# Filler ahead of each recurrence, a norm in steps, and two projections on other PSUM banks

## The chip, the cores and the metric

The kernel runs on one core of a Trainium2 chip. The core has TensorE (PE, matrix products and transposes into PSUM), VectorE (DVE), ScalarE (ACT), GpSimd (POOL) and SyncE (SP), which issues the DMAs. Each engine runs its own instructions in order and waits for the others by semaphores. The metric is the time of one execution on the device in microseconds (us). PSUM, where TensorE writes, has eight banks; each holds a tile of 128 partitions x 512 float32.

## The reference

Two blocks run one after the other on a sequence of 1024 rows of 1024 columns. The change lies in the first part of the first block and at the beginning of its second part:

```python
def hybrid_mixer(h, w_in, ..., w_out):
    z = h @ w_in
    qkv, gate, a_logit, b_logit, cfm_in = jnp.split(z, [s1, s2, s3, s4], axis=-1)
    qkv = jax.nn.silu(causal_dwconv(qkv, gdn_conv_w))
    ...
    o = gated_delta_rule_chunked(q, k, v, g, beta)
    o = rmsnorm(o, gdn_norm_g) * jax.nn.silu(gate)
    c = jax.nn.glu(cfm_in, axis=-1)
    c = causal_dwconv(c, cfm_dw_w) + cfm_dw_b
    c = jax.nn.silu(layernorm(c, cfm_ln_g, cfm_ln_b))
    return jnp.concatenate([o_gdn, c], axis=-1) @ w_out

def memory_cross_attention(h, mem_n, w_q, w_kv, w_o):
    q = (h @ w_q).reshape(B, T, XATTN_HEADS, XATTN_HEAD_DIM)
    k, v = jnp.split(mem_n @ w_kv, 2, axis=-1)
    ...

y = hybrid_mixer(rmsnorm(h, g[0]), ...);  h = h + rmsnorm(y, g[1])
y = memory_cross_attention(rmsnorm(h, g[2]), rmsnorm(mem, mem_norm_g[l]), ...)
```

A gated linear unit with a short convolution and a second block of two more recurrences follow; they are the same in both kernels.

## The kernel before

**Products.** A float32 product is made of three matmuls on operands split into a high and a low part (`mm3`, L184 to L186): high by high, high by low, low by high, each 128 x 128 by 128 x 512. Activations are split as `x` (hi and lo), weights by `wunits`: a load of 512 KB on SP's queue brings `raw` (two buffers), ACT casts the high part `whi` (L149) and POOL, or VectorE in some places, subtracts to get `wlo` (L150), six buffers each. Each load gives two k-slices of a panel. At most LOOK = 3 loads are prepared ahead.

**PSUM.** The eight banks are four tagged `pa` (`A()`), two tagged `pm` (`M()`), and one each for `M(ns=0)` and `M(ns=1)`, which the trace shows as `pm` too. A projection panel takes four banks, one for each row tile (or column tile), and holds them over eight k-slices. Transposes of row norms go through the two banks of `M()`: `rows_to_T` transposes four 128x128 blocks into a bank (L229), ACT casts them to the high part and VectorE subtracts the low part. `banks()` returns the four of `A()` and the four others in turn.

**Stage 1.** The sequence is worked on in two halves of 512 rows (h = 0, 1), the four heads of the recurrence in two pairs (u = 0, 1). `weave(main, f, rate)` runs a recurrence `gdn_(h, u)` and takes `rate` filler steps of the generator `f` for each of its steps; what is left of the filler is then run to its end. A filler step of a projection is one `mm3`. A recurrence begins with squares of q and k (L551 on ACT), their sums by products with a column of ones (L553, 128x1), inverse roots in small steps on VectorE (L132 to L137), transposes (L571, L572) and decay products (L575); L459 gives the running sums of the log decay `glog` for both pairs of a half, in `s1_decay`. Its inputs come from `s1_qkv`: projections, a four-tap filter on VectorE (L385) and an activation (L386). The causal filter of 31 taps is L491 on VectorE. At the end of a recurrence L663 to L673 update the state and write the output.

**The order.** The program is written in one sequence, but a scheduler reorders it before it runs: it takes the written order as the priority, and for each engine puts next what it believes to be ready and to have a free buffer. The outcome is one fixed order for each engine.

**After the last recurrence** come the output projection of the first half (`out_`, two panels), its residual norm (`resid`: sums of squares L233, then L295 and L296), the row norm for the attention (`norm_T`: L308, then `rows_to_T`, 32 transposes), the output projection of the second half, whose two panels are copied out by L727, and `kv`, the projections of the memory to keys (two panels, 128x256 matmuls) and values (two panels, two row tiles each), which are split into `e` and `vl` by L149 and L150.

## Time and profile before

| | |
|---|---|
| median of 3 runs | 2958.16 us (2957.79 to 2959.43) |
| profiled execution | 2965.35 us, span 2963.5 us |
| mean granted clock of TensorE | 0.981 |
| busy: PE | 2806.0 us, 95% of the span |
| busy: DVE, POOL, ACT | 1778.4, 1241.0, 1125.8 us |
| DMA | 286.81 MB, mean 97 GB/s |

The profiled execution is one run; its trace gives the rows below. A row of the timeline has the start and the length of an instruction (or of a run of like ones, with its count), and in brackets how long the engine had been idle ahead of it and what ended that. A window's row has how long PE was busy in it and the granted clock as a share of full speed: 1.00 is the upper of two levels (2.4 GHz), 0.50 would be the lower one (1.2 GHz) throughout. Stage 1 lies between 0 and about 670 us: gdn(0,0) starts near 80 us, gdn(0,1) near 205, gdn(1,0) near 347, gdn(1,1) near 500; the output projection of the second half runs from 617 to 670, the keys and values from 675 to 731.

### The profile page before, as it was taken

Reading aid. Unit: us, or ns where it says so; the run is one execution under the profiler, and the core shown is the slowest. Engines: PE = TensorE matmul, PEld = TensorE weight load, DVE = VectorE, ACT = ScalarE, POOL = GpSimd, SP = SyncE. Lnnn points to the kernel's source line nnn. Section 1 sums busy time; section 2 is a strip of 40 time slices with the busy share of each in tenths; the row PEclk is TensorE's granted clock in tenths of the full one; section 3 lists DMA queues with packets and bytes.
Section 4 is the critical chain, followed back from the end, with each engine's and each line's share of the span. In section 5 each row is a group of like instructions: output and inputs, shape, how many; then the busy total and the mean of one; then the engine's idle time right before and its main releaser. Section 6 shows DMA issues by size and latency. Waiting matters only on the chain.

```text
span 2963.5 us, 40689 instructions
## 1 busy us (share of the span) xinstructions
PE 2806.0 (95%) x15268; PEld 2280.1 (77%) x15268; DVE 1778.4 (60%) x3525; ACT 1125.8 (38%) x2264; POOL 1241.0 (42%) x915
## 2 busy tenths in 40 slices
PE   7999998998999989999899998999999999999998
PEld 6787887877877778887688886777777777777776
DVE  6597789765345775546854547646546365464444
ACT  4443544555444443334333333323234322232333
POOL 3332333233342555554455543344443533434443
PEclk9999999999999999999899999999999999999999
DMA  4122111146242733334333234122223332222222
GB/s 152 43 65 72 50 44 58 36 136 199 70 136 83 244 113 94 99 93 160 129 98 100 91 94 160 61 86 65 86 79 99 93 123 70 79 61 90 79 78 100
DMA packets 136709, 286.81 MB, mean 97 GB/s; under 512 B 9793, under 2 KB 12865, under 8 KB 136513
## 3 DMA queue, kind: packets, MB, share of 16 engines
q1 hardware_dynamic: 136512, 284.22, 30.0%
q8 instruction: 120, 1.97, 0.3%
q14 instruction: 77, 0.62, 0.1%
HBM read 265.83 MB, written 18.35 MB: 96 GB/s over the span
## 4 chain that ended last, share of the span: by engine, by line
PE 52%; DVE 11%; DMA 3%; ACT 2%; issue 1%; POOL 1%; SPq 0%; ACTq 0%; DVEq 0%; POOLq 0%
PE pa L184 12%; PE pa L185 11%; PE pa L186 11%; PE pm L184 4%; PE pm L185 4%; PE pm L186 4%; PE pm L966 2%; DMA r<-h 1%; POOL wlo L150 1%; DMA wad<-in_w_ada 1%; DVE fo L833 1%; DVE mac L876 1%; DVE e L295 1%; PE pm L1023 0%; PE pm L1022 0%
## 5 line engine op out<-in xcount | busy, mean ns | idle before, releaser
L150 POOL TENSOR_TENSOR wlo<-raw,whi 128x512 fp32r<-128x512 f32 (+1 forms) x792 | 1145.8, 1453 | 1637.2 <-ACT whi L149 1614.0
L149 ACT CAST whi<-raw 128x512 fp32r<-128x512 f32 (+1 forms) x808 | 496.6, 620 | 1116.9 <-PE pa L186 515.8
L184 PE MATMUL pa<-whi,x 128*128 128x512 f32 (+2 forms) x1408 | 554.9, 395 | 12.8 <-DVE rt L1066 3.9
L186 PE MATMUL pa<-whi,x 128*128 128x512 f32 (+2 forms) x1408 | 546.2, 388 | 0.0
L185 PE MATMUL pa<-wlo,x 128*128 128x512 f32 (+2 forms) x1408 | 545.2, 387 | 0.0
L184 PE MATMUL pa<-x,whi 128*128 128x512 f32 x1024 | 428.5, 419 | 17.9 <-ACT x L1152 13.7
L185 PE MATMUL pa<-x,whi 128*128 128x512 f32 x1024 | 413.2, 403 | 0.0
L186 PE MATMUL pa<-x,wlo 128*128 128x512 f32 x1024 | 412.7, 403 | 0.0
L184 PEld LDWEIGHTS pa<-whi,x 128*128 128x128 f32 x1408 | 265.2, 188 | 75.2 <-issue 7.0
L186 PEld LDWEIGHTS pa<-whi,x 128*128 128x128 f32 x1408 | 265.1, 188 | 52.9 <-issue 0.9
L185 PEld LDWEIGHTS pa<-wlo,x 128*128 128x128 f32 x1408 | 265.4, 188 | 50.8 <-issue 1.4
L184 PEld LDWEIGHTS pa<-x,whi 128*128 128x128 f32 x1024 | 196.4, 192 | 58.3 <-ACT x L1152 14.5
L186 PEld LDWEIGHTS pa<-x,wlo 128*128 128x128 f32 x1024 | 195.9, 191 | 42.9
L185 PEld LDWEIGHTS pa<-x,whi 128*128 128x128 f32 x1024 | 196.6, 192 | 34.3 <-DVE x L150 0.4
L491 DVE SCALAR_TENSOR_TENSOR e<-padc,cw,e 128x512 f32<-128x512 f32 x240 | 202.4, 880 | 0.1
L828 DVE COPY fh<-pad 128x2 f32<-128x2 f32 x88 | 32.3, 367 | 227.3 <-ACT pad L826 227.3
L833 DVE SCALAR_TENSOR_TENSOR fo<-pad,cols,fo 128x512 f32<-128x512 f32 x176 | 159.8, 936 | 0.7
L184 PE MATMUL pm<-x,whi 128*128 128x512 f32 x384 | 154.5, 403 | 0.0
L185 PE MATMUL pm<-x,whi 128*128 128x512 f32 x384 | 152.9, 398 | 0.0
L186 PE MATMUL pm<-x,wlo 128*128 128x512 f32 x384 | 152.7, 398 | 0.0
L150 DVE TENSOR_TENSOR x<-pm,x 128x512 fp32r<-128x512 f32 x112 | 75.4, 687 | 66.4 <-ACT x L149 66.0
L149 ACT CAST x<-pm 128x512 fp32r<-128x512 f32 x112 | 64.6, 589 | 71.1 <-PE pm L229 42.6
(360 smaller groups left out, 4485.9 us busy)
## 6 DMA issues: line engine op xcount, KB each, us to landing
raw<-in_w_in SPq DMA_DIRECT2D x112, 512.0 KB, 3.9
raw<-in_ffn_w_up SPq DMA_DIRECT2D x88, 512.0 KB, 3.9
raw<-in_ffn_w_down SPq DMA_DIRECT2D x44, 512.0 KB, 3.9
raw<-in_w_out SPq DMA_DIRECT2D x32, 512.0 KB, 4.0
raw<-in_w_qf SPq DMA_DIRECT2D x32, 512.0 KB, 3.9
h<-e SPq DMA_DIRECT2D x48, 256.0 KB, 3.2
r<-h SPq DMA_DIRECT2D x24, 512.0 KB, 4.6
wad<-in_w_ada SPq DMA_DIRECT2D x24, 512.0 KB, 4.1
```

The lines of the kernel that those rows point to most:

```text
L149: self.nc.scalar.copy(hi, src)
L150: (lo_eng or self.nc.vector).tensor_tensor(lo, src, hi.bitcast(F32), ALU.subtract)
L184: mm(ps, lhsT=lh, rhs=rh, start=first, stop=False)
L185: mm(ps, lhsT=lh, rhs=rl, start=False, stop=False)
L186: mm(ps, lhsT=ll, rhs=rh, start=False, stop=last)
L295: nc.vector.scalar_tensor_tensor(yt, yt, r[:, t : t + 1], g[:, c], ALU.mult, ALU.mult)
L491: v.scalar_tensor_tensor(o, pad[:, k : k + HT], w(k), o, ALU.mult, ALU.add)
L828: v.tensor_copy(fh[:, i, :], pad[:, HT:])
L833: v.scalar_tensor_tensor(o, pad[:, k : k + HT], self.col(k0 + k), o, ALU.mult, ALU.add)
L876: v.scalar_tensor_tensor(ac, w, sc[:, k : k + 1], ac, ALU.mult, ALU.add)
L966: mm(pm[64 * e : 64 * e + 64, c, :], lhsT=kG[:, s], rhs=q[:, s], start=True, stop=True)
```

## The change

Four things are changed, all in the code that issues stage 1 and `kv`.

- `weave` gets a `lead`: so many steps of the filler are taken before the recurrence's first step. It is 8 for gdn(0,0) and 10 for gdn(0,1) and gdn(1,0); gdn(1,1) has none. With it, the decay (`s1_decay`) is no longer computed with the projection of its inputs but at the head of `gdn_(h, 0)`.
- The row norm of the second half of x, a call of `load_norm` ahead of gdn(0,1), becomes a generator `norm_steps`, of which one step is taken for every three steps of `conv_(0, 1)`.
- The first panel of the second half's output projection goes to the two banks of `M()` and those of `M(ns=0)` and `M(ns=1)` instead of `A()`.
- The four panels of `kv` take `banks()`, the two sets in turn, instead of `A()` each time.

```diff
+def beside(f, g, n):
+    for i, _ in enumerate(f):
+        yield
+        if i % n == n - 1:
+            next(g, None)
+    run(g)
...
-def weave(main, f, rate):
+def weave(main, f, rate, lead=0):
+    for _ in range(lead):
+        next(f, None)
     due = 0.0
...
-        return self.s1_decay(g) + (bt,)
+        return g, bt
...
-    def out_stream(self, y, xh, xl):
-        ps = [self.A() for _ in range(NTT)]
+    def out_stream(self, y, xh, xl, ps=None):
+        ps = ps or [self.A() for _ in range(NTT)]
...
-            ps = self.proj_T(units, xh, xl, nt=256)
+            ps = self.proj_T(units, xh, xl, nt=256, ps=self.banks())
...
-            ps = self.proj_R(units, xh, xl, ntt=2)
+            ps = self.proj_R(units, xh, xl, ntt=2, ps=self.banks())
...
             def gdn_(h, u):
+                if u == 0:
+                    dec[h] = self.s1_decay(dec[h][0]) + dec[h][1:]
                 yield from self.gdn(u, qkv[h, u], dec[h], gate[h])
 
             run(qkv_(0, 0, x))
-            weave(gdn_(0, 0), fill(conv_(0, 0, x), qkv_(0, 1, x)), RATE[0])
-            xn = self.load_norm(a["x"][HT:, :], gb(0))
-            weave(gdn_(0, 1), fill(conv_(0, 1, x), qkv_(1, 0, xn)), RATE[1])
-            weave(gdn_(1, 0), fill(conv_(1, 0, xn), norm_(0), conv_(1, 1, xn), qkv_(1, 1, xn)), RATE[2])
+            weave(gdn_(0, 0), fill(conv_(0, 0, x), qkv_(0, 1, x)), RATE[0], 8)
+            xn = self.X(), self.X()
+            norm = self.norm_steps(a["x"][HT:, :], gb(0), *xn)
+            weave(gdn_(0, 1), fill(beside(conv_(0, 1, x), norm, 3), qkv_(1, 0, xn)), RATE[1], 10)
+            weave(gdn_(1, 0), fill(conv_(1, 0, xn), norm_(0), conv_(1, 1, xn), qkv_(1, 1, xn)), RATE[2], 10)
             weave(gdn_(1, 1), fill(mix_(0), out_(0), norm_(1)), RATE[3])
             weave(mix_(1), out_(0), 4)
             self.resid(0, y[0], 0, 1)
             xa = self.norm_T(y[0], gb(2))
-            run(out_(1), out_(1))
+            run(out_(1, [self.M(), self.M(), self.M(ns=0), self.M(ns=1)]), out_(1))
...
+    def norm_steps(self, src, g, xh, xl):
+        hs = []
+        for t in range(NTT + 1):
+            if t < NTT:
+                hs.append(self.R())
+                self.nc.sync.dma_start(hs[t], src[t * P : (t + 1) * P, :])
+                self.prenorm([hs[t]], g, None, None)
+                yield
+            if t:
+                hr = hs[t - 1]
+                self.rows_to_T([hr[:, :HT], hr[:, HT:]], xh, xl, t - 1)
+                yield
```

The lines from L75 to L727 that are named here have numbers 11 higher in the changed kernel.

**PE at the start of gdn(0,1).** The long matmuls (`pa`, 128x512) are filler; L571 and L572 are the recurrence's first transposes (L582 and L583 in the changed kernel), L553 its sums of squares (now L564), L229 the norm's transposes (now L240). Before:

```order
L185 MATMUL pa<-x_131,whi 128x512
L186 MATMUL pa<-x_130,wlo 128x512
L184 MATMUL pa<-x_130,whi 128x512
L185 MATMUL pa<-x_131,whi 128x512
L572 MATMUL pm<-ident,e_252 128x128
L571 MATMUL pm<-ident,e_1159 128x128
L186 MATMUL pa<-x_130,wlo 128x512
L184 MATMUL pa<-x_130,whi 128x512
L229 MATMUL pm<-ident,r_1954 128x128 x4
L185 MATMUL pa<-x_131,whi 128x512
```

After, from the point where 26 long matmuls in a row have gone ahead:

```order
L240 MATMUL pm<-ident,r_1942 128x128 x2
L195 MATMUL pa<-x_130,whi 128x512
L196 MATMUL pa<-x_131,whi 128x512
L197 MATMUL pa<-x_130,wlo 128x512
L564 MATMUL pm<-ones,cv 128x1 x8
L195 MATMUL pa<-x_130,whi 128x512
L196 MATMUL pa<-x_131,whi 128x512
L197 MATMUL pa<-x_130,wlo 128x512
L564 MATMUL pm<-ones,cv 128x1 x4
L582 MATMUL pm<-ident,e_1124 128x128
L583 MATMUL pm<-ident,e_252 128x128
L582 MATMUL pm<-ident,e_1124 128x128
```

The transposes of the recurrence stood ahead of its sums of squares and among the norm's; now they stand behind the first of these sums, and long matmuls lie in between.

**VectorE ahead of gdn(1,1).** L491 are the taps of the causal filter (L502 in the changed kernel), L385 those of the four-tap filter that the recurrence's inputs wait for (now L396), L132 to L137 the small steps of an inverse root for the end of gdn(1,0) (now L143 to L148). Before:

```order
L135 TENSOR_TENSOR tn<-tn 128x8
L491 SCALAR_TENSOR_TENSOR e_3359<-padc,cw,e_3359 128x512
L136 SCALAR_TENSOR_TENSOR tn<-tn,gn 128x8
L491 SCALAR_TENSOR_TENSOR e_3359<-padc,cw,e_3359 128x512
L137 SCALAR_TENSOR_TENSOR tn<-tn 128x8
L491 SCALAR_TENSOR_TENSOR e_3359<-padc,cw,e_3359 128x512
L135 TENSOR_TENSOR tn<-tn 128x8
L379 COPY pad_4794<-hist 128x3
L491 SCALAR_TENSOR_TENSOR e_3359<-padc,cw,e_3359 128x512
L136 SCALAR_TENSOR_TENSOR tn<-tn,gn 128x8
L380 COPY hist<-pad_4785 128x3
L385 SCALAR_TENSOR_TENSOR x_4213<-pad_4785,cols,x_4213 128x512
```

After, from the last output sum of gdn(1,0) on:

```order
L689 TENSOR_TENSOR e_2457<-e_2457,pm 128x256
L706 SCALAR_TENSOR_TENSOR gn<-gn 128x8
L391 COPY hist<-pad_4785 128x3
L390 COPY pad_4794<-hist 128x3
L143 TENSOR_SCALAR tn<-gn 128x8
L502 SCALAR_TENSOR_TENSOR e_3297<-padc,cw,e_3297 128x512
L144 TENSOR_SCALAR tn<-tn 128x8
L396 SCALAR_TENSOR_TENSOR x_4151<-pad_4785,cols,x_4151 128x512
L146 TENSOR_TENSOR tn<-tn 128x8
L391 COPY hist<-pad_4794 128x3
L396 SCALAR_TENSOR_TENSOR x_4151<-pad_4785,cols,x_4151 128x512
```

Between the end of gdn(1,0) and the first L385 stand ten taps L491 before, and one now.

**PE at the first panel of the second half's output projection.** The long matmuls with `x_5704` are this projection, L229 (L240) the transposes of `norm_T(y[0])`. Before, in the second panel:

```order
L184 MATMUL pa<-whi,x_5704 128x512
L229 MATMUL pm<-ident,r_6021 128x128 x4
L185 MATMUL pa<-wlo,x_5704 128x512
L229 MATMUL pm<-ident,r_6021 128x128 x4
L186 MATMUL pa<-whi,x_5705 128x512
L184 MATMUL pa<-whi,x_5704 128x512
L185 MATMUL pa<-wlo,x_5704 128x512
L186 MATMUL pa<-whi,x_5705 128x512
L184 MATMUL pa<-whi,x_5704 128x512
L185 MATMUL pa<-wlo,x_5704 128x512
L229 MATMUL pm<-ident,r_6038 128x128 x4
L186 MATMUL pa<-whi,x_5705 128x512
```

After, in the first panel:

```order
L197 MATMUL pm<-whi,x_5705 128x512
L195 MATMUL pm<-whi,x_5704 128x512
L196 MATMUL pm<-wlo,x_5704 128x512
L197 MATMUL pm<-whi,x_5705 128x512
L240 MATMUL pm<-ident,r_6021 128x128 x8
L240 MATMUL pm<-ident,r_6038 128x128 x8
L240 MATMUL pm<-ident,r_6055 128x128 x8
L240 MATMUL pm<-ident,r_6072 128x128 x8
L195 MATMUL pm<-whi,x_5704 128x512
L196 MATMUL pm<-wlo,x_5704 128x512
L197 MATMUL pm<-whi,x_5705 128x512
L195 MATMUL pm<-whi,x_5704 128x512
```

The transposes went in by fours among the matmuls of the second panel on the `pa` banks; now all 32 stand in one piece, 36 matmuls into the first panel, and its other 60 stand behind them.

## Rows read from the trace of the kernel before

**Rows 1.** Page, part 1: busy time of each engine, share, instructions.
```profile
PE 2806.0 (95%) x15268; PEld 2280.1 (77%) x15268; DVE 1778.4 (60%) x3525; ACT 1125.8 (38%) x2264; POOL 1241.0 (42%) x915
```

**Rows 2.** Waits of PE, 0 to 1000 us: total, times, longest.
```profile
PE pm L572 <- ACT e L386: 6.1, 2, 4.3
PE pa L184 <- DVE e L150: 4.7, 2, 4.1
PE pm L572 <- ACT x L386: 4.0, 1, 4.0
PE pm L575 <- DVE Vs L581: 3.8, 3, 2.3
...
PE pa L184 <- DVE vl L150: 2.8, 1, 2.8
```

**Rows 3.** Ten-us windows, PE: length, PE busy, granted clock, DMA share, GB/s.
```profile
90.00:100.00 10.00, 10.00 (x36) 0.62 0.00 0
200.00:210.00 10.00, 7.18 (x46) 1.00 0.23 74
210.00:220.00 10.00, 8.51 (x34) 0.66 0.34 106
220.00:230.00 10.00, 7.18 (x31) 0.86 0.27 66
...
350.00:360.00 10.00, 10.00 (x45) 0.51 0.16 51
500.00:510.00 10.00, 6.03 (x46) 0.69 0.02 5
640.00:650.00 10.00, 6.74 (x36) 1.00 0.65 212
690.00:700.00 10.00, 7.88 (x43) 0.66 0.77 239
```

**Rows 4.** Timeline of PE, start of gdn(0,0): start, us, instruction [idle before].
```profile
85.47 0.40 PE L459 MATMUL pm<-glog,tri 128*128 128x16 f32 x2 [1.23 <-DVE glog L450]
```

**Rows 5.** Timeline of ACT, start of gdn(0,1).
```profile
210.81 0.63 ACT L386 ACTIVATE e<-e 128x512 f32<-128x512 f32 x1 [4.30 <-DVE e L385]
```

**Rows 6.** Timeline of PE, start of gdn(1,0).
```profile
347.78 1.90 PE L553 MATMUL pm<-ones,cv 128*128 128x1 f32 x16
```

**Rows 7.** Timeline of VectorE, start of gdn(1,1).
```profile
504.29 0.74 DVE L491 SCALAR_TENSOR_TENSOR e<-padc,cw,e 128x512 f32<-128x512 f32 x1
...
505.10 0.74 DVE L385 SCALAR_TENSOR_TENSOR x<-pad,cols,x 128x512 f32<-128x512 f32 x1
```

**Rows 8.** Timeline of PE, output projection of the second half.
```profile
641.78 0.50 PE L184 MATMUL pa<-whi,x 128*128 128x512 f32 x1 [2.29 <-ACT e L727]
...
644.77 0.63 PE L229 MATMUL pm<-ident,r 128*128 128x128 f32 x4 [1.10 <-DVE r L308]
...
669.27 0.39 PE L184 MATMUL pa<-whi,x 128*128 128x512 f32 x1
...
669.97 0.39 PE L184 MATMUL pa<-whi,x 128*128 128x512 f32 x1
```

**Rows 9.** Timeline of VectorE, output projection of the second half.
```profile
623.84 1.26 DVE L133 TENSOR_SCALAR tn<-tn 128x4 int32<-128x4 int32 x1
...
630.49 1.41 DVE L295 SCALAR_TENSOR_TENSOR e<-e,tn,gb 128x512 f32<-128x512 f32 x2
...
633.02 4.18 DVE L295 SCALAR_TENSOR_TENSOR e<-e,tn,gb 128x512 f32<-128x512 f32 x3
...
655.53 1.36 DVE L150 TENSOR_TENSOR x<-pm,x 128x512 fp32r<-128x512 f32 x2 [0.92 <-ACT x L149]
```

**Rows 10.** Timeline of POOL, the same stretch.
```profile
632.13 2.15 POOL L150 TENSOR_TENSOR wlo<-raw,whi 128x512 fp32r<-128x512 f32 x1 [4.43 <-ACT whi L149]
```

**Rows 11.** Timeline of ACT, values' projection.
```profile
722.52 1.15 ACT L149 CAST whi<-raw 128x512 fp32r<-128x512 f32 x2 [2.26 <-DMA raw<-in_xa_w_kv]
726.30 1.14 ACT L149 CAST whi<-raw 128x512 fp32r<-128x512 f32 x2 [2.63 <-DMA raw<-in_xa_w_kv]
```

More of the change, by code (lines that the diff above doesn't have):

```diff
@@ L1318, in mix_, with out_ @@
                 yield from self.s1_mix(gate[h], *m[h])
-            def out_(h):
-                yield from self.out_stream(y[h], *m[h])
+            def out_(h, ps=None):
+                yield from self.out_stream(y[h], *m[h], ps)
             def gdn_(h, u):
+                if u == 0:
+                    dec[h] = self.s1_decay(dec[h][0]) + dec[h][1:]
                 yield from self.gdn(u, qkv[h, u], dec[h], gate[h])
             run(qkv_(0, 0, x))
-            weave(gdn_(0, 0), fill(conv_(0, 0, x), qkv_(0, 1, x)), RATE[0])
-            xn = self.load_norm(a["x"][HT:, :], gb(0))
-            weave(gdn_(0, 1), fill(conv_(0, 1, x), qkv_(1, 0, xn)), RATE[1])
-            weave(gdn_(1, 0), fill(conv_(1, 0, xn), norm_(0), conv_(1, 1, xn), qkv_(1, 1, xn)), RATE[2])
+            weave(gdn_(0, 0), fill(conv_(0, 0, x), qkv_(0, 1, x)), RATE[0], 8)
[3 more added lines that the diff above has]
+            weave(gdn_(1, 0), fill(conv_(1, 0, xn), norm_(0), conv_(1, 1, xn), qkv_(1, 1, xn)), RATE[2], 10)
             weave(gdn_(1, 1), fill(mix_(0), out_(0), norm_(1)), RATE[3])
```

## Prediction

> **What bounds the kernel now.** I read the page's busy shares first: TensorE (PE) is busy for 95% of the span [rows 1], so the time can only move where PE waits, where it runs at the lower of its two clock levels, or where the change makes it wait. The list of PE's waits over the first millisecond, which holds stage 1, was next [rows 2]: the waits at the recurrences' first transposes (L572, one of 4.3 and one of 4.0 us), at its decay products (L575) and at the key and value projections (L184 waiting for `e` and for `vl`). Third came PE's busy time and granted clock in slices of 10 us [rows 3]: what a slice lacks to 10 us is idle, and one minus the granted clock, times 10 us, is the work lost to the lower level (1.2 instead of 2.4 GHz). The four starts show as pits there: idle 2.8, 1.5 and 2.8 us around the start of gdn(0,1) with clocks of 0.66 and 0.86 behind it, a clock of 0.51 at gdn(1,0), 4.0 us idle at 0.69 at gdn(1,1), a clock of 0.62 at gdn(0,0). Last I read the timeline of the output projection, where the change swaps banks. PE is in order, so the order of its instructions before and after says who stands behind whom; the durations are from the trace.
>
> The profiled execution took 2965.35 us, 7.2 us more than the median of 2958.16. The sum is made against the former, and the same difference is then carried to the median. Minus is a gain.
>
> **gdn(0,0), lead of 8.** No instruction is added by a lead; 8 steps of three matmuls, 0.70 us each by the distance of two steps [rows 8], go ahead of the recurrence. But the bottleneck there is a chain on ACT and VectorE: L459 waited 1.23 us for `glog` at 85.47 [rows 4], and both engines' orders up to it are the same in both kernels. 25 long matmuls stood ahead of L459, now 27 do. So PE will have done the same work when `glog` comes, and its two short waits (1.8 us, what the first row of [rows 2] leaves beside its 4.3, and 1.23) become one longer one. The clock falls there already (0.62 in the next slice, 3.8 us lost). I take +1 us, with ends of −1 and +3. The moved s1_decay is the same two matmuls and exponentials, issued a little later; it is in this number.
>
> **gdn(0,1), lead of 10, and the second half's norm in steps.** Today L572 waits 4.3 us for the cast-and-activate L386, which waited 4.30 us for the taps L385 on VectorE [rows 2, 5]: the taps stand mixed with the row norm and the causal filter. The norm's own transposes make the other 2.8. In the new order, 26 long matmuls stand between the last product of gdn(0,0) and the first instruction of gdn(0,1), the transposes come in twos and eights among them, and L572 comes behind the squares. The norm's loads, squares, scalings and 32 transposes are the same ones, its four loads still early on the queue of SP; nothing is added. Of the 7.1 us idle I leave 1, so −6. Of the 4.8 us that 0.66 and 0.86 stand for, I take 3 back, since the short 128x1 products L553 still come in a bunch there. Sum −9, ends −5 (a new wait of a microsecond or two, no clock) and −12 (all of it).
>
> **gdn(1,0), lead of 10.** There the clock fell with no wait ahead of it: 16 products L553 ran for 1.9 us from 347.78 [rows 6] and the slice behind them was granted 0.51, worth 4.9 us. The lead puts long matmuls between them in four groups instead of one bunch. Against this, the end of gdn(0,1) has used up its filler earlier: 17 small groups now stand among 30 matmuls, and the 2.3 us for `Vs` (L575) stays, because that chain on VectorE is unchanged. I take 40% of the clock and nothing else, −2; ends −5 (all the clock) and +2 (waits among the bare groups, as L575's other two in [rows 2], 1.5 us together).
>
> **gdn(1,1), no lead.** PE's rows are nearly the same, but the filler taps L491 that VectorE ran up to 504.29 stood ahead of the recurrence's L385 at 505.10 [rows 7]; about ten of them did, now one does. So the 4.0 us for `x` from L386 go; the clock of 0.69 I leave, as 32 products L553 run just ahead of that wait. −4, ends −2 and −6.
>
> **Output projection of the second half, first panel on the four other banks.** Here the change costs. Two of these banks come from `M()`, the pair through which the 32 transposes of `norm_T(y[0])` go, and those are issued first. In PE's new order only the 36 matmuls of two row tiles and six k (as many as there are split weight buffers) stand ahead of the transposes; then come all 32 transposes, then the other 60 and the second panel's 96. Before, 96 matmuls ran beside the norm and the transposes went in between the next panel's. From the rows: the second panel started at 641.78 after 2.29 us of waiting, so the first panel's 96 matmuls at 0.232 us began at 617.2 [rows 8]. Now PE stops at 617.2 + 36 x 0.232 = 625.6. The transposes began at 644.77, set by VectorE. They will begin earlier, because POOL runs dry of weights to split: L295 x3 took 4.18 us where x2 took 1.41, beside a split of 2.15 us on POOL, and a tiny operation took 1.26 us, as a second one did 1.20, where the eleven others of that chain take under 0.2 [rows 9, 10]. Without these hits it is 4.2 us less, and 1.2 us of weight casts leave ACT's queue ahead of the squares: 644.8 − 5.4 = 639.4. From there to the last split took 12 us (655.53 + 1.36), of which the first waiting matmul needs seven eighths and POOL's quiet saves one or two: 9 us, so 648.4. Then 156 matmuls, 36.2 us, to 684.6, and one fall of the clock as the slice at 690 shows it, 3.4 us [rows 3]: 688.0 against 670.4 (669.97 and what is left of its step). **+17.5 us**. Ends: 14 with the clock up, 24.5 if the transposes begin at 644.8 and take 10.5 us. Behind PE, ACT's weight casts now queue behind the squares and the eight casts of the transposes, so k6 and k7 are split only at about 653; PE wants them at 657, so that costs nothing, and would cost up to 3 us if the transposes ended 4 us sooner.
>
> **Keys and values on banks in turn.** The wait of 4.1 us for `e` (bank not yet split out), the low clock after it (0.66, 3.4 us) and 2.8 us for `vl` have no cause any more: 10.3 us at the most. But weights then become the limit: ACT's casts at 722.52 and 726.30 waited for their loads and are 3.8 us apart, for 2 x 6 matmuls, 2.8 us of PE [rows 11]. Everything of the queue moves up a few us with the faster casts ahead, not all. I take 6 of 10.3; ends 3 (the last wait alone) and 9. Behind this point PE's order is the same in both kernels.
>
> **Sum**: +1 − 9 − 2 − 4 + 17.5 − 6 = −2.5. 2965.35 − 2.5 = 2962.9; less 7.2, **2955.7 us**. All lower ends together are −19 and all upper ends +19.5.
>
> **Rivals.**
> *The bank swap is cheap.* If VectorE goes even faster with POOL quiet, and the transposes keep the clock up, the swap costs 14; with the better halves of the rest (−11 at gdn(0,1), −3 at gdn(1,0), −8 at the keys) the sum is −11, **2947 us**. For it: the slice at 640 shows a full clock in spite of waits of 2.3 and 1.1 us in it [rows 3, 8]. Against: PE would be idle for 13 us on end, and a wait of 4.1 us was enough for 0.66 at 690.
> A sharper form is that PE loses nothing there: if the first panel's matmuls on free banks covered the norm as they do now, the sum would be −20, **2938 us**. The Trainium skill, Perfetto Trace Analysis, section Matmuls, states this as its rule: independent matmul groups should rotate through different PSUM banks, so that the evacuation of one overlaps the next group. By that rule the swap is a gain. The trace agrees at the keys (4.1 us waiting for a bank); here the order of PE speaks against it, since the other banks are not free: I give it 2%.
> *The clock stays down at the starts (slower).* The mechanism is the short products at the head of each recurrence: the clock fell behind L553 with no idle at all at 347.78, so removing waits need not bring it back. Then gdn(0,1) gives −6, gdn(1,0) 0, gdn(0,0) costs 3, the keys give −4 and the swap costs a second partial fall, 19: −2.5 + 3 + 2 + 2 + 2 + 1.5 = +8, **2966 us**. It decides from +5.9, 8.4 us above the forecast: two falls of 3.4 to 4.9 us that I took as gone or never counted. For it: the slice of 0.51. Against: at gdn(0,1) today's two low slices stand each beside a wait, of 4.3 and 2.8 us.
> The Trainium skill, TensorE: Matmul & The Clock Gate, section HAM oscillation, ties falls to idle gaps; by that rule the leads, which close gaps, would bring all of the clock back at gdn(0,1), 1.8 us more than I take, and the sum would be −4.3. The row at 347.78 differs from it, as no gap precedes that fall.
> *The leads do nothing*: had the order already held filler ahead of each recurrence, gdn(0,1) and gdn(1,1) would stay and the sum be +10.5, 2969 us. At gdn(0,0) it is nearly so; at gdn(0,1) the order shows 26 long matmuls ahead. 3%.
>
> **How the numbers follow.** Forecast 53% (its own range 2950 to 2961), cheap swap 22%, no loss at the swap 2%, clock down 20%, leads void 3%. A difference under 0.2%, 5.9 us, is about what a measurement of this kernel can tell from none. Below 2952.2 lie most of the cheap swap (0.19), the 0.02 and a quarter of the forecast (0.13): 0.34. Above 2964.1 lie three quarters of clock down (0.15), the void leads (0.03) and 0.03 of the forecast: 0.21. Between: 0.45. The range from 2943 to 2968 leaves out the 2% below, the lowest 0.04 of the cheap swap, and, above, the void leads and a quarter of clock down (0.08).
>
> **What would show it.** Of the changed trace: PE idle from about 625 to 639, minus the gains ahead of it, with 32 transposes in one piece behind and the next long matmul on a bank `pm` waiting for a split; no 4 us wait at the first transposes of gdn(0,1) and gdn(1,1); clock in the slices behind the starts of gdn(0,1) and gdn(1,0); no wait for `e` or `vl` in the keys, waits for `wlo` or `whi` instead. The prediction is wrong if PE stops for less than 10 us or more than 25 at the swap, or if the stretch from gdn(0,1) to the end of out_(0) is not 12 to 18 us shorter.

## The result

The changed kernel took 2979.18 us (median of 4 runs, 2976.26 to 2979.49) beside 2958.8 us for the kernel before on the same chip: a ratio of 1.0057 with a 95% interval of 1.0045 to 1.0069, so 13 to 20 us slower (the two medians are 20.4 us apart). The forecast was 2955.7 us, about equal, and the range ended at 2968. The profiled execution of the changed kernel took 2979.49 us (span 2977.7), 14.1 us more than that of before; PE's busy time rose by 7 us with the same number of instructions [rows 1]:

```profile
PE 2813.1 (94%) x15268; PEld 2278.8 (77%) x15268; DVE 1784.6 (60%) x3525; ACT 1131.2 (38%) x2266; POOL 1245.0 (42%) x915
```

PE's waits over the first millisecond, the answer to [rows 2], show what became of the waits named in the prediction (L572 is L583 now): the one of 4.3 us at gdn(0,1) is gone, the one of 1.8 at gdn(0,0) is 1.9, the one of 4.0 at gdn(1,1) became 1.3, the two of the keys and values are gone, and a new one of 16.3 us stands at the top. Inside the recurrences, the wait for `Xm` has grown from 2.3 us to 7.0. Before:

```profile
PE pm L631 <- DVE Xm L627: 2.3, 5, 0.7
```

After:

```profile
PE pm L240 <- DVE r L319: 17.2, 2, 16.3
...
PE pm L642 <- DVE Xm L638: 7.0, 7, 2.5
...
PE pm L586 <- DVE Vs L592: 3.6, 3, 2.4
...
PE pm L196 <- POOL wlo L161: 2.0, 3, 0.9
PE pm L583 <- ACT e L397: 1.9, 1, 1.9
...
PE pm L583 <- ACT x L397: 1.3, 1, 1.3
```

Ten-us windows of PE after, to be read beside [rows 3] (length, busy, granted clock, DMA share, GB/s):

```profile
90.00:100.00 10.00, 10.00 (x44) 0.66 0.01 2
200.00:210.00 10.00, 10.00 (x58) 1.00 0.13 37
210.00:220.00 10.00, 10.00 (x51) 0.66 0.38 122
220.00:230.00 10.00, 9.03 (x57) 1.00 0.33 105
350.00:360.00 10.00, 10.00 (x56) 1.00 0.17 49
500.00:510.00 10.00, 7.17 (x27) 0.50 0.18 52
620.00:630.00 10.00, 1.80 (x8) 0.81 0.57 174
630.00:640.00 10.00, 1.86 (x8) 0.50 0.54 199
640.00:650.00 10.00, 7.88 (x29) 0.50 0.28 79
```

At gdn(0,1) the idle time is nearly gone (7.1 us became 1.0). At gdn(1,1) the clock got worse (0.69 to 0.50), and between 620 and 640 PE did almost nothing. Followed along PE's order, the changed kernel is 3.9 us ahead when the first panel of the second half's output projection begins (617.2 before by the prediction's working, 613.3 after by the row of its first matmul), 15.2 us behind at the first matmul of the keys (675.31 to 690.53), 8.7 behind in the middle of the query projection (at 758), and from there to the end, where both kernels run the same order, it loses another 5.5 us in small steps.

### The profile page after: what moved, and what is told of

It is laid out like the page before. It is cut to its first block, busy times and chain, and to the rows that moved or that the text cites. A ratio compares the mean times of both kernels' runs of the same rounds, so it can differ in the third digit from the quotient of the medians.

```text
span 2977.7 us, 40668 instructions
## 1 busy us (share of the span) xinstructions
PE 2813.1 (94%) x15268; PEld 2278.8 (77%) x15268; DVE 1784.6 (60%) x3525; ACT 1131.2 (38%) x2266; POOL 1245.0 (42%) x915
## 4 chain that ended last, share of the span: by engine, by line
PE 67%; DVE 22%; DMA 3%; ACT 3%; issue 3%; POOL 1%; SPq 0%; ACTq 0%; DVEq 0%; POOLq 0%
PE pa L195 15%; PE pa L196 14%; PE pa L197 14%; DVE e L502 5%; PE pm L196 4%; PE pm L195 4%; PE pm L197 4%; PE pm L977 2%; DMA r<-h 1%; ACT junk L244 1%; DVE e L306 1%; DVE x L396 1%; DMA wad<-in_w_ada 1%; POOL wlo L161 1%; DVE e L307 1%
## 5 line engine op out<-in xcount | busy, mean ns | idle before, releaser
L195 PE MATMUL pa<-whi,x 128*128 128x512 f32 (+2 forms) x1376 | 543.1, 396 | 10.5 <-DVE rt L1077 3.9
L197 PE MATMUL pa<-whi,x 128*128 128x512 f32 (+2 forms) x1376 | 533.7, 388 | 0.0
L196 PE MATMUL pa<-wlo,x 128*128 128x512 f32 (+2 forms) x1376 | 532.4, 387 | 0.0
L195 PEld LDWEIGHTS pa<-whi,x 128*128 128x128 f32 x1376 | 259.5, 189 | 71.1 <-issue 7.0
L197 PEld LDWEIGHTS pa<-whi,x 128*128 128x128 f32 x1376 | 259.5, 189 | 51.8 <-issue 0.9
L502 DVE SCALAR_TENSOR_TENSOR e<-padc,cw,e 128x512 f32<-128x512 f32 x240 | 210.6, 915 | 0.1
L240 PE MATMUL pm<-ident,r 128*128 128x128 f32 x240 | 44.8, 325 | 52.8 <-DVE r L319 29.0
```

The costliest lines, as they stand in the source:

```text
L195: mm(ps, lhsT=lh, rhs=rh, start=first, stop=False)
L196: mm(ps, lhsT=lh, rhs=rl, start=False, stop=False)
L197: mm(ps, lhsT=ll, rhs=rh, start=False, stop=last)
L240: nc.tensor.transpose(pm[:, i, :], pieces[j][:, i * P : (i + 1) * P], self.ident)
L502: v.scalar_tensor_tensor(o, pad[:, k : k + HT], w(k), o, ALU.mult, ALU.add)
```

## Experiments on the banks

All edits are to the kernel before or to the changed kernel, and every ratio is to runs of the kernel before on the same chip.

**The swap alone** (`e1_only_swap`, on the kernel before):

```diff
-            run(out_(1), out_(1))
+            run(out_(1, [self.M(), self.M(), self.M(ns=0), self.M(ns=1)]), out_(1))
```

> The kernel before with one edit: the first panel of the second half's output projection on the four other banks. Theory 1 (PE's order: 36 matmuls, then all 32 transposes, then the rest): PE idle for about 16 us ahead of the transposes, out projection 20 us longer, time about 2979 us, so that this edit alone makes the whole difference of the changed kernel. Rival (the swap's stop is long only because the starts ahead of it are changed, or part of it is given back later): 2962 to 2972 us.

Measured: 1.0066 (1.0053 to 1.0079), 16 to 23 us. The wait is the same as in the changed kernel. Timeline of PE, columns as in [rows 4]:

```profile
639.34 1.94 PE L229 MATMUL pm<-ident,r 128*128 128x128 f32 x8 [16.34 <-DVE r L308]
```

The keys' first matmul stood at 691.47 (675.31 before). So the swap alone makes all of the loss, and the starts ahead of it have no part in it.

**The swap with the transposes elsewhere** (`transposes_on_pa`, on the changed kernel; `norm_T` hands the pool on to `rows_to_T`):

```diff
-            xa = self.norm_T(y[0], gb(2))
+            xa = self.norm_T(y[0], gb(2), ps=self.A)
```

> The changed kernel with one edit: the 32 transposes of norm_T(y[0]) go through the four pa banks instead of the two pm banks, so that the first panel of the out projection shares no bank with them (its 96 matmuls stand in one piece in PE's order, then the transposes, then the second panel). Theory 1 (the shared pair of banks puts the transposes into the middle of the panel): PE does not stop at 36 matmuls, the swap costs 20 us less the part of the norm that 96 matmuls do not cover (some 5 us of idle before the transposes and 6 to 8 us in them), time 2966 to 2972 us. Rival (a panel on those four banks is slow in itself, or the norm is slower there): 2975 us or more.

Measured: 1.0013 (1.0004 to 1.0022), against 1.0057 for the changed kernel. The panel's 96 matmuls now run to their end, and PE waits 5.2 us for the norm instead of 16.3, then little by little for the scaled rows. Timeline of PE:

```profile
643.68 2.82 PE L240 MATMUL pa<-ident,r 128*128 128x128 f32 x12 [5.18 <-DVE r L319]
648.73 1.12 PE L240 MATMUL pa<-ident,r 128*128 128x128 f32 x4 [2.23 <-DVE r L319]
```

Against the changed kernel without the swap (`e4_all_but_swap`, below) that is still 0.0023 or some 7 us, the part of the norm that nothing covers. It is the pair of banks shared with the transposes that made the rest (the transposes also have four banks here instead of two; no run separates that).

**The keys and values alone** (`e2_only_kv`, on the kernel before, the two lines of `kv`):

> The kernel before with one edit: keys and values on the two sets of banks in turn. Theory 1 (the waits for banks go, the weights' loads take half of it back): 6 to 8 us faster, 2951 to 2953 us. Rival (loads bound this stretch, so that a wait for weights takes the place of each wait for a bank): within 3 us of before.

Measured: 0.9988 (0.9979 to 0.9997), 3.6 us, between the theory and its rival. No bank is waited for any more, but the weights are: waits for `wlo` and `whi` of 0.2 to 2.0 us follow one another, 6 us in sum between 672 and 765. Two of them, in the timeline of PE:

```profile
706.37 0.50 PE L185 MATMUL pa<-wlo,mxh 128*128 128x512 f32 x1 [0.85 <-POOL wlo L150]
...
723.76 0.63 PE L185 MATMUL pm<-wlo,mxh 128*128 128x512 f32 x1 [2.00 <-POOL wlo L150]
```

**Everything but the swap** (`e4_all_but_swap`, on the changed kernel):

> The changed kernel with the first panel of the second half's output projection back on its old banks. Theory 1 (the swap costs 20 us and the rest gains 11): 2948 to 2952 us. Rival (starts cost, keys gain): 2958 us.

Measured: 0.9990 (0.9981 to 0.9999), 2960.1 us. That is the gain of the keys alone. With the starts alone at 1.0000 (below), the three parts add up: 19.6 − 3.6 + 0 = 16.0 us, against 17 for the whole change.

**The second panel instead of the first on the four other banks** (`second_panel_kv`, on the kernel before with the keys and values in turn):

```diff
-            run(out_(1), out_(1))
+            run(out_(1))
+            run(out_(1, [self.M(), self.M(), self.M(ns=0), self.M(ns=1)]))
```

> The kernel before with the keys and values on banks in turn, and the out projection's second panel instead of the first on the four other banks; no leads, no steps. Theory 1: the wait of 2.3 us for the second panel's banks goes, the keys give 3.6 us as measured alone, nothing is stopped by the transposes: 5 to 7 us faster than the kernel before. Rival (the transposes' pair of banks holds up two of the second panel's four row tiles as it did the first's): slower than before.

Measured: 0.9998 (0.9988 to 1.0007); the gain of the keys does not show, though the interval overlaps that of the keys alone. The theory was wrong here. With the second panel off the `pa` banks PE waits 4.7 us for the norm where it waited 2.3 us for those banks and 1.1 for the norm [rows 8]. And the panel must leave its banks before the transposes of the memory's norm can have them: these now wait 3.2 us for the copies L727. Timeline of PE:

```profile
643.27 0.63 PE L229 MATMUL pm<-ident,r 128*128 128x128 f32 x4 [4.73 <-DVE r L308]
...
672.71 0.66 PE L229 MATMUL pm<-ident,r 128*128 128x128 f32 x4 [3.22 <-ACT e L727]
```

The same edit with the starts (`second_panel_all`) gave 1.0008 (0.9997 to 1.0018).

> The changed kernel with the out projection's second panel on the four other banks instead of its first. Theory 1 and 2 (starts 0, keys 3.6, swap's 20 us gone, wait of 2.3 us gone): 5 to 6 us faster than the kernel before and equal to second_panel_kv within 2 us. Rival (starts gain once the swap is away): 3 us or more faster than second_panel_kv.

So a bank that is free for the next panel is not free for what comes after it: each of the two turns only moved the wait to the next user of `M()`.

## Experiments on the starts

**The starts alone** (`e3_starts_only`: leads, later decay, norm in steps; no edit of banks):

> The leads, the later decay and the norm in steps, without the two edits of banks. Theory 1, by the two traces (idle and clock at the four starts 12 us better, 5 us of new waits within the recurrences): the out projection begins 4 us sooner, 2955 us. Rival, by the medians (the changed kernel is 20 us slower, of which the swap makes 20 and the keys give back 7): the starts cost, 2965 us.

Measured: 1.0000 (0.9991 to 1.0009). The 14 us that the prediction took from the starts did not come at all. Wider windows of PE say where the gain at gdn(0,1) went. Before:

```profile
200.00:250.00 50.00, 41.84 (x221) 0.90 0.31 100
250.00:330.00 80.00, 77.29 (x514) 1.00 0.16 48
330.00:380.00 50.00, 45.23 (x259) 0.90 0.14 45
380.00:490.00 110.00, 104.72 (x658) 1.00 0.17 52
490.00:530.00 40.00, 34.49 (x208) 0.87 0.18 53
```

The starts alone:

```profile
200.00:250.00 50.00, 48.20 (x283) 0.93 0.32 98
250.00:330.00 80.00, 75.06 (x474) 1.00 0.17 52
330.00:380.00 50.00, 44.73 (x254) 0.86 0.13 43
380.00:490.00 110.00, 103.27 (x642) 1.00 0.18 53
490.00:530.00 40.00, 34.87 (x201) 0.87 0.13 40
```

At gdn(0,1) (200 to 250) idle time fell from 8.2 to 1.8 us. The body of gdn(0,1) behind it lost 2.2 us more than before, the body of gdn(1,0) (380 to 490) 1.5 more, and the starts of gdn(1,0) and gdn(1,1) won next to nothing in idle time and had no better clock.

**Is it the norm or the lead?** (`steps_no_lead`: all leads at 0.)

```diff
-            weave(gdn_(0, 1), fill(beside(conv_(0, 1, x), norm, 3), qkv_(1, 0, xn)), RATE[1], 10)
+            weave(gdn_(0, 1), fill(beside(conv_(0, 1, x), norm, 3), qkv_(1, 0, xn)), RATE[1], 0)
```

> The later decay and the norm in steps, with all leads at 0, without the edits of banks. Theory 1: the wait of 2.8 us behind the norm's chain goes and the wait of 4.3 us at the first transposes of gdn(0,1) goes too, if it was the norm that stood among the taps: 4 to 7 us of idle time less at gdn(0,1), and the time as for the starts alone, 2960 to 2963 us. Rival (the leads carry the gain at gdn(0,1)): both waits as before there.

Measured: 1.0004 (0.9995 to 1.0014). Idle time between 200 and 250 us was 3.9 us, so the norm in steps with the later decay brings two thirds of what they bring with the leads; and the time does not show it either.

**Less filler inside** (`slow_rate_starts`: the starts alone, with `RATE = (0.75, 0.9, 1.0, 0.55)`):

> The kernel with leads, decay and norm in steps, without the edits of banks, and with the rates of filler within the recurrences lowered to 0.75, 0.9 and 1.0 from 0.9, 1.1 and 1.2, so that what is left for after a recurrence grows. Rival (filler used up too soon): waits inside the recurrences move from their ends to all of their length, time within 3 us of the starts alone or up to 6 us faster. Theory 2 (VectorE): the recurrences' chain of small steps has less filler beside it, PE waits more, 2 to 8 us slower than the starts alone.

Measured: 1.0006 (0.9998 to 1.0015). In PE's order in this kernel's trace 48 long matmuls stand between the last product of gdn(0,0) and the first of gdn(0,1), and 224 between the first and the last of gdn(0,1); in the starts alone 29 and 253, with no lead 6 and 279, before 9 and 276. So what is put ahead of a recurrence lacks in it. The idle time does not follow these counts, though: from 250 to 330 us it is 2.7 us with the slow rate, 4.9 in the starts alone, 2.7 before, and from 200 to 250 us 6.9, 1.8 and 8.2. What one stretch gains another loses: over 70 to 620 us the four orders (before, starts, no lead, slow rate) are idle for 35.2, 32.3, 32.7 and 34.4 us.

**VectorE's part.** VectorE was busy for 105.6 of the 110 us from 380 to 490 in the starts alone (99.2 before), which suggested that it gives the gain back. I left out 14 of the causal filter's 31 taps, in the kernel before and with the starts:

```diff
-                for k in range(30):
+                for k in range(14, 30):
```

> The kernel before with 16 of the 31 taps of the causal filter computed (14 taps left out for each of 8 column tiles: 112 operations of about 0.72 us on VectorE, some 80 us of its work in stage 1). To be read against few_taps_starts. If VectorE holds PE up inside the recurrences, PE's waits there fall: 5 to 12 us faster than before. If not, within 3 us of before.

> The same 16 taps in the kernel with leads, decay and norm in steps, without the edits of banks. Theory 2 (in the bodies of the recurrences VectorE is busy 96 to 99% and gives back what the starts gain): with less work on VectorE the leads keep their gain, and this is 6 to 12 us faster than few_taps_before. Rival (the leads take filler that then lacks within the recurrences, whatever VectorE does): equal to few_taps_before within 3 us.

Measured: 0.9997 (0.9989 to 1.0006) without the starts, 0.9971 (0.9961 to 0.9981) with them, so the starts are worth 0.26% here, as theory 2 said. The traces bear out its mechanism in one of two places only. Windows of PE in few_taps_before:

```profile
250.00:330.00 80.00, 78.58 (x529) 1.00 0.17 54
...
380.00:490.00 110.00, 104.65 (x651) 1.00 0.18 53
```

In few_taps_starts:

```profile
250.00:330.00 80.00, 76.05 (x479) 1.00 0.16 47
...
380.00:490.00 110.00, 104.61 (x659) 0.98 0.18 54
```

From 250 to 330 us VectorE's busy time fell to 57 of 80 us with the starts (79 with all taps), and yet idle time of PE there rose against few_taps_before from 1.4 to 4.0 us, as it does with all taps. From 380 to 490 us VectorE's busy time fell from 105.6 to 93.3 us with the starts, and the 1.5 us of idle time that they cost PE there with all taps are gone (5.4 in both). What fell most was the time lost to the lower clock, from 21.9 to 11.4 us over 70 to 620, in a profiled execution that was 7.4 us faster than its kernel's median. So a saturated VectorE is not what gives the gain back in gdn(0,1); for gdn(1,0) that stays open.

**The clock.** The rest of the loss in stage 1, beside the idle time, is the clock: 17 us before, 19 in the starts alone. To see whether the short products L553 bring it down, I left 12 of the 16 out (`few_sums`, on the kernel before; one product with four columns for each square):

```diff
-            for c in range(NTT):
-                mm(pn[:, c, j : j + 1], lhsT=sq[:, c * P : (c + 1) * P], rhs=self.ones[:, 0:1], start=True, stop=True)
+            mm(pn[:, j, 0:4], lhsT=sq[:, j * P : (j + 1) * P], rhs=self.ones[:, 0:4], start=True, stop=True)
```

> The kernel before with 4 instead of 16 products with ones at the head of each recurrence (L553; the sums of squares are then not those of the rows, the squares themselves are all computed). If that bunch of short products brings the clock down at the starts, the slices behind it at gdn(1,0) and gdn(1,1) are granted 0.9 or more instead of 0.51 and 0.69, and the time is 5 to 12 us less. If the waits do, the clock at gdn(0,1) and gdn(1,1) stays as it is, and the time is 2 to 5 us less (the products left out).

Measured: 0.9949 (0.9936 to 0.9961), 15 us. The greater part of that can be the products themselves: the trace has two records for each product, so 96 records are left out, and 16 took 1.90 us in [rows 6], which gives up to 11 us as an estimate. What bears on the clock are the windows behind the starts of gdn(0,0) and gdn(1,0), to be read beside 0.62 and 0.51 in [rows 3]:

```profile
90.00:100.00 10.00, 7.73 (x46) 1.00 0.19 55
...
350.00:360.00 10.00, 7.36 (x43) 1.00 0.18 52
```

Every wait at these two starts was still there, and as PE got through the products sooner it waited for `Vs` at gdn(0,0) as well. Timeline of PE at gdn(0,0), the wait ahead of the products and the one behind them:

```profile
85.48 0.40 PE L459 MATMUL pm<-glog,tri 128*128 128x16 f32 x2 [1.20 <-DVE glog L450]
...
95.90 0.68 PE L574 MATMUL pm<-tri,glog 128*128 128x128 f32 x4 [2.27 <-DVE Vs L580]
```

So at these two starts the kernel before fell to the lower level behind the products and not behind a wait, as the rival of the prediction had it. At gdn(1,1), where PE waits 5.3 us in this kernel, the clock still fell.

With the starts added (`few_sums_starts`):

> The leads, decay and norm in steps, without the edits of banks, with 4 instead of 16 products with ones at each recurrence's head (sums of squares not those of the rows). To be read against few_sums, 0.51% faster than before. Theory 2 (VectorE in the bodies): equal to few_sums within 3 us. Rival (the clock behind the short products ate the starts' gain): 5 us or more faster than few_sums.

Measured: 0.9984 (0.9976 to 0.9993), slower than few_sums by 0.35%. At the first matmul of the keys this kernel was 1.3 us behind few_sums (659.66 and 658.34), at the end of the span 8.9 us (2954.0 and 2945.1; the medians are 4.9 us apart): most of the difference arose in the later stages, whose order the edits do not touch. As in the result itself, I can't say what makes it.

## Wide products

The same sums can be had without single columns. Each product is written 128 columns wide, and each lands one column behind the last, so that the column that counts is left standing (`wide_sums`, on the kernel before):

```diff
-        pn = self.M([P, 4, 4])
+        pw = self.M()
+        pn = pw[:, :16].rearrange("p (j c) -> p c j", j=4)
...
-                mm(pn[:, c, j : j + 1], lhsT=sq[:, c * P : (c + 1) * P], rhs=self.ones[:, 0:1], start=True, stop=True)
+                i = 4 * j + c
+                mm(pw[:, i : i + P], lhsT=sq[:, c * P : (c + 1) * P], rhs=self.ones, start=True, stop=True)
```

> The kernel before with all 16 products with ones, each written 128 columns wide instead of 1, into overlapping stretches of one bank so that the column that is needed is the one left standing. Same count and same weight loads as L553. If it is the single columns of that bunch that bring the clock down at gdn(0,0) and gdn(1,0), the slices at 90 and 350 are granted 0.9 or more there and the time is 5 to 9 us less, the wider products' own 2 us per recurrence already taken off. If the count of short instructions does, the slices stay at 0.62 and 0.51 and the time is 2 to 8 us more.

> The same wide products, and the keys and values on banks in turn. Were both gains to add: 3.6 us less than wide_sums, 9 to 12 us less than the kernel before. If the clock does not stay up: 0 to 5 us more than the keys alone.

> The changed kernel with the wide products and with the out projection's first panel on its old banks. Theory 2 (what the starts gain is given back in the bodies, where VectorE is busy throughout): equal to wide_sums_kv within 3 us. Rival (the starts' gain went to the clock that falls behind the short products): 5 us or more faster than wide_sums_kv.

The clock stayed up at both starts, with the same count of products and with the waits ahead of them still there. Windows of PE in wide_sums:

```profile
90.00:100.00 10.00, 7.66 (x45) 1.00 0.17 52
...
350.00:360.00 10.00, 9.78 (x56) 1.00 0.01 2
```

At gdn(1,0) PE's order is not the same, though: the products, two records each, stand in groups of 2 to 10 records among others, before in groups of 16, 8 and 8. Over all twenty traces gdn(0,0) is the clear case: from 86 to 96 us the granted clock is 0.56 to 0.73 in the thirteen kernels with one-column products, and 0.94 to 1.00 in the seven with few or with wide ones. At gdn(1,0), from 350 to 360 us, the changed kernel was granted 1.00 with one-column products, and few_sums_starts 0.83 without them, with a wait of 2.5 us in that window.

The timeline of wide_sums at gdn(0,0), the wait ahead of the products and the products:

```profile
85.70 0.40 PE L459 MATMUL pm<-glog,tri 128*128 128x16 f32 x2 [1.20 <-DVE glog L450]
...
86.17 3.91 PE L555 MATMUL pm<-ones,cv 128*128 128x128 f32 x32
```

The 32 records of the products took 3.91 us at the upper level; before, the first 16 took 2.33 us and the other two groups of 8 took 1.70 each. And yet the time was the same, 1.0001 (0.9991 to 1.0011): time lost to the clock over 70 to 620 us fell from 17 to 8 us, and idle time rose from 35 to 41.5, with a wait of 7.1 us for the same L386 at gdn(1,1) that was 4.0 us before. Waits of PE in wide_sums, columns as in [rows 2]:

```profile
PE pm L574 <- ACT x L386: 7.1, 1, 7.1
...
PE pm L574 <- ACT e L386: 6.1, 2, 4.3
```

PE came sooner to chains that are not its own (at gdn(0,0) it waited 2.3 us for `Vs`, as in few_sums). With the keys in turn it was 0.9993 (0.9985 to 1.0002), with the starts as well 0.9971 (0.9960 to 0.9982): 2954.57 us beside 2962.79. With the wide products the leads and the steps do pay, 0.22%, and the first matmul of the keys moves from 675.15 to 667.68. Two more runs split them.

> Wide products, keys and values on banks in turn, the norm in steps and the later decay, all leads at 0. To be read between wide_sums_kv (0.9993 of before) and wide_sums_starts_kv (0.9971). If the norm in steps makes the gain: 0.997 to 0.998, idle time in 200 to 250 us near 4 us. If the leads do: 0.999 or more, and the keys begin at 672 us or later.

> Wide products, keys and values on banks in turn, the leads and the later decay, the second half's norm in one piece as before. If the leads make the gain: 0.997 to 0.998, keys begin at 666 to 669 us. If it takes the norm in steps: 0.999 or more.

Measured: 0.9983 (0.9974 to 0.9992) with the steps alone, keys at 671.48; 0.9975 (0.9964 to 0.9985) with the leads alone, keys at 670.31. Each is worth some 4 us and both together 7.5 by the position of the keys; the intervals of the three times overlap. Stage 1 in numbers (70 to 620 us; lost to the clock is one minus the granted clock, times busy time, summed over windows of 5 us; each row is one profiled execution, and these lie up to 7.4 us off their kernel's median):

| kernel | idle, us | lost to the clock, us | keys begin at |
|---|---|---|---|
| before | 35.2 | 16.8 | 675.3 |
| starts alone | 32.3 | 19.2 | 677.2 |
| steps, no lead | 32.7 | 16.3 | 675.2 |
| few taps / with starts | 26.5 / 23.9 | 21.9 / 11.4 | 672.4 / 659.3 |
| few sums / with starts | 39.7 / 35.0 | 5.2 / 8.4 | 658.3 / 659.7 |
| wide sums, keys | 39.6 | 9.6 | 675.2 |
| the same with steps | 37.8 | 6.5 | 671.5 |
| the same with leads | 34.4 | 7.0 | 670.3 |
| the same with both | 31.6 | 8.1 | 667.7 |

The last row is the fastest of the versions that leave nothing out: the changed kernel without the swap and with wide products, 8 us (5 to 12) faster than before. The pair few sums does not fit the table's story, in which the starts pay once the clock is up: there idle time fell by 4.7 us, 3.2 of it went to the clock, and the keys began no sooner. What decides when filler put ahead of a recurrence is worth its place is therefore settled only in part.

## Why the prediction was wrong, step by step

By the runs the starts gave 0 us instead of −14, the swap +19.6 instead of +17.5, and the keys and values −3.6 instead of −6. Of the 18.5 us between the two sums 14 are the starts, so that is the step that failed: time won at each start was counted as won at the end.

**gdn(0,0), +1 us.** Small, and of the wrong sign: idle 3.8 us and clock 5.0 from 75 to 105 before, 2.1 and 4.8 after, a gain of 2 where the better end was −1. The two short waits did not become one longer one; one of 1.9 us was left, and `glog` came in time. In the starts alone L470 (L459 before) waited 1.1 us for it again, and the gain was 0.7.

**gdn(0,1), −9 us.** The mechanism held at the place: idle time from 200 to 250 us fell by 6.4 us in the starts alone, and the wait of 4.3 us at L583 is gone. The step that failed is the one that let this count for the end. The sum held each start by itself, as if a matmul put ahead of a recurrence were not missed inside it. In the starts alone idle time rose by 2.2 us inside gdn(0,1) and by 1.5 inside gdn(1,0), the time lost to the clock rose by 2.4, and the keys began no sooner. That the idle time rose because matmuls were missed fits the counts of long matmuls (276 inside gdn(0,1) before, 253 with the starts) and the wait for `Xm`, but is not shown: the slow rate has the fewest, 224, and was idle for no longer than before from 250 to 330 us.

**gdn(1,0), −2 us.** The prediction took 40% of one fall of the clock. (Its "16 products" at 347.78 are 16 records of 8 products, and the other 8 stood behind them in two groups, not in one bunch.) That fall is not steady. The kernels e2_only_kv and second_panel_kv run the same order as before up to far behind this place, and from 330 to 380 us the clock was 0.90 before (the row stands above), 0.86 and 0.97 in these two, at the same busy time: a spread of 5 us. The window in e2_only_kv:

```profile
330.00:380.00 50.00, 45.25 (x246) 0.86 0.13 43
```

And in second_panel_kv:

```profile
330.00:380.00 50.00, 45.20 (x280) 0.97 0.14 43
```

With the leads it was between 0.86 and 0.97 too, over five kernels. The 0.97 of the changed kernel's own trace can therefore not be counted as a gain of the change. The Trainium skill, TensorE: Matmul & The Clock Gate, section What's actually happening, says that the chip's look at PE's activity runs freely and does not begin anew with a kernel; these rows fit it, and so does the spread of the kernel before, 2955.8 to 2969.9 us over all its runs on several chips, but no run here shows that it is the cause.

**gdn(1,1), −4 us.** The taps moved as the order said, and the wait fell from 4.0 to 1.3 us, but PE's next work (the transposes of the mix, then L716) ran at 0.50 instead of 0.69, and waits of 0.7 us followed. Over the 25 us from the first sum of squares on, idle time fell from 5.1 to 2.9 us and the time lost to the clock rose from 3.1 to 5.4. Removing a wait in a stretch at the lower level only moved work into it.

**The swap, +17.5 us.** Right in mechanism and place, and 2 us short in size (19.6 measured alone). Timeline of PE in the changed kernel:

```profile
620.95 0.39 PE L195 MATMUL pm<-whi,x 128*128 128x512 f32 x1
...
638.14 1.94 PE L240 MATMUL pm<-ident,r 128*128 128x128 f32 x8 [16.35 <-DVE r L319]
...
647.75 1.09 PE L240 MATMUL pm<-ident,r 128*128 128x128 f32 x4 [0.90 <-DVE r L319]
648.49 0.78 PE L195 MATMUL pm<-whi,x 128*128 128x512 f32 x1
```

PE stopped 36 matmuls in, and the transposes began 24.8 us after the panel did (22.2 predicted), the next long matmul 35.2 us after it (31.2 predicted). Of the missing microseconds, 1.6 is a wait of VectorE for a load that the prediction had not seen, and POOL was quiet as it said. Timeline of VectorE in the changed kernel, the wait for the load:

```profile
632.37 1.29 DVE L307 TENSOR_TENSOR e<-e,r 128x512 f32<-128x512 f32 x2 [1.64 <-DMA r<-in_x]
```

Timeline of POOL, 36.8 us without a split:

```profile
653.46 5.64 POOL L161 TENSOR_TENSOR wlo<-raw,whi 128x512 fp32r<-128x512 f32 x4 [36.76 <-ACT whi L160]
```

**Keys and values, −6 us.** The term that was mis-sized: 3.6 us. The weights took back more than half of the 10.3 us, as the waits for `wlo` in e2_only_kv show.

**The rivals.** The rival "the clock stays down at the starts" named the right products, and its sum of +8 was nearer than the forecast, but it too kept 6 us at gdn(0,1). It got a chance of 20%, on the ground that the low slices at gdn(0,1) stand beside waits; the fall at 347.78, with no wait in the 7 us ahead of it, was the row to give more weight. The rule of the Trainium skill, Perfetto Trace Analysis, section Matmuls (independent groups rotate through the banks), held for the keys (3.6 us) and not for the out projection, where the other banks belong to work that stands ahead.

**From the profile to the median.** The profiled execution of before was 7.2 us above its median, and I carried that difference over. The changed kernel's profiled execution was 0.3 us above its own. One trace of before is one draw from a spread of some 10 us; the 7.2 us were no constant.

## What to carry to other kernels

Filler is a stock: before crediting work that is moved ahead of a stall, look at the place that it is taken from, and count idle time and clock over both. Before a panel is sent to other banks, read in the engine's order who else holds them and stands ahead; transposes that share a pair of banks with half a panel put their own chain in the middle of it. Where the clock falls without a wait, look at the instructions just ahead of it, and change them before the waits around them; that may still not shorten the time (1.0001 with the wide products alone).

## What was not expected of the hardware

At gdn(0,0) PE fell to its lower level behind a bunch of 8 one-column products without a pause between them (16 records, 2.33 us in the kernel before) in all thirteen kernels that have them (0.56 to 0.73 from 86 to 96 us), and did not behind 16 products of 128 columns in the same place (1.00), whatever waits stood around them. At gdn(1,0) the same was seen in before (0.51) and in wide_sums (1.00), but not in every kernel. Kernels whose order is the same from some point on still differed there by up to 7.6 us by the end of the span (few_sums and few_sums_starts), and the kernel before by more than 10 us from run to run. Beside splits on POOL, the three scalings L295 at 633 took 4.18 us on VectorE [rows 9]; with POOL quiet, the same three took 2.07 in the changed kernel. Timeline of VectorE there (L306 is L295 before):

```profile
626.64 2.07 DVE L306 SCALAR_TENSOR_TENSOR e<-e,tn,gb 128x512 f32<-128x512 f32 x3
```
